# Dealing out the later groups' queries by half heads, sharing the first look-ups, and a list in two parts

## The chip, the core and the metric

The kernel runs on one core of one Trainium2 chip. The metric is the device time of one execution in microseconds. The core has five engines with a queue each: TensorE (PE: matmuls; PEld is its loading of weights), VectorE (DVE), ScalarE (ACT), GpSimd (POOL) and SyncE (SP, which here only issues DMAs). Sixteen DMA engines move the data. An engine works off its queue in order.

## The reference, cut to what matters

One layer: a modulated projection, a two-way matrix-memory scan beside attention, an output projection and a layer norm, and then a PEER layer (a product-key mixture of 16384 tiny experts) on 512 tokens. Only the PEER layer is touched by the change:

```python
q = (xt @ wq).reshape(P_BLOCK, P_HEADS, 2, P_HALF)      # 8 heads x 2 halves of 128 columns
s = jnp.einsum('nhpd,hpkd->nhpk', q, keys)              # scores against 128 keys each
s1, i1 = lax.top_k(s[:, :, 0], P_TOPK); s2, i2 = lax.top_k(s[:, :, 1], P_TOPK)
cand_s = (s1[..., :, None] + s2[..., None, :]).reshape(P_BLOCK, P_HEADS, P_TOPK * P_TOPK)
cand_i = (i1[..., :, None] * N_KEYS + i2[..., None, :]).reshape(P_BLOCK, P_HEADS, P_TOPK * P_TOPK)
top_s, pos = lax.top_k(cand_s, P_TOPK)
idx = jnp.take_along_axis(cand_i, pos, axis=-1).reshape(P_BLOCK, P_HEADS * P_TOPK)
g = jax.nn.softmax(top_s.astype(jnp.float32), axis=-1).reshape(P_BLOCK, P_HEADS * P_TOPK).astype(xt.dtype)
act = jax.nn.gelu(jnp.einsum('nd,ned->ne', xt, u[idx]), approximate=False)
return jnp.einsum('ne,ned->nd', g * act, v[idx])
```

It is done for four groups of 128 tokens.

## The kernel before

**Queries and scores.** `scores(t0, ...)` makes the scores of two groups at a time. It is a generator over 16 "heads" (8 heads x 2 halves) and one step more: a step multiplies `wq`'s 128 columns with `h2T` (8 passes over k, line 839, 16 matmul instructions as the trace counts them), copies the query to `qT` (line 841), and takes the scores of the head before (line 847). For groups 0 and 1 it runs through at once. For groups 2 and 3 it is the generator `sc1`, whose scores go through a tile `sc_` of two buffers (`to_memory`, lines 862 to 865: a copy on ScalarE, then a DMA on SP to `scd` in memory). Its last six heads read weights that lie in the three `uv` buffers of the pool `eb` (`late_rows`).

**Selection.** `select(t)` finds each token's experts on VectorE (max, index, replace; lines 896 to 980) and leaves row, column and weight in `iig`. It uses the large tile `work` as scratch. `parts` holds a later group's scores, loaded from `scd`.

**Prelude.** `prelude(t)` turns `iig` into a table of which token uses which expert, and from it into lists of rows. Three transposes `ptr` (line 1001) come first. Sixteen chunks follow (lines 1014 to 1034): VectorE builds one-hot matrices `A` and `B`, TensorE multiplies them (24 matmuls a chunk: `pf` counts, `pW` weights), ScalarE writes the weights to `work`. Then SP writes `work` to the memory table `Wd` in 16 pieces of 512 KB (line 1038; for group 0 all are sent there). From `pf` come the tables (`tables`, twice: F1 marks experts that one token uses, up to 12 blocks of 128, F2 all others), and from the tables the list: `look_up` goes through the 29 blocks in groups of three (LB): a comparison on VectorE, three matmuls `ppk`, two small VectorE instructions, and for each block a Sign on ScalarE whose accumulated sum counts how many entries lie below (line 1095). The first 12 blocks are looked up first, then tables F2, then the other 17. When all are done, three VectorE instructions (lines 1115 to 1117) make the two integer tables `ri` and `wi` of the whole list.

**The order ahead of the blocks.** A loop runs `select(0)` and `prelude(0)`, 49 steps, and after each step whose number is in HEADS it takes one step of `sc1`:

```python
    for i, _ in enumerate(chain(select(0, work), prelude(0))):
        if i in HEADS:
            next(sc1, None)
    for _ in sc1:
        pass
```

Steps 0 to 19 are the selection, 20 to 35 the chunks, 36 the first tables, 37 to 40 and 42 to 47 look-ups, 41 the second tables.

**The blocks.** `blocks` works off 4 x 29 blocks of 128 rows in a software pipeline (PIPE): `rows` gathers a block's 128 rows of `uv` (1 MB, line 1122 on GpSimd, seven buffers) and its part `wr` of `Wd`; a block of the first 12 gathers its tokens (`xg`) and takes dot products on VectorE (line 1183), one of the other 17 is transposed (`put`, line 1287) and multiplied densely (`s`, line 1301), a gelu on ScalarE and a product `wt` on VectorE (line 1303); then `py` (line 1211) adds the block up on TensorE. The order of a group's blocks is `seqs`: for groups 0 to 2 it begins with three blocks of the second part. While a group's blocks run, `select` and `prelude` of the next group are dealt out in between by a table of costs (`cost`).

The order in an engine's queue is fixed when the kernel is built, by a scheduler of the framework which starts from the order of the text and may draw an instruction forward past others that it takes to be waiting.

Of the kernel before, what the change touches and what calls it, by code (L numbers as in the profile page):

```python
# [11 lines left out]
F16 = mybir.dt.float16  # L12
I32 = mybir.dt.int32
# [6 lines left out]
P = 128  # L20
# [42 lines left out]
HEADS = (2, 4, 6, 8, 10, 12, 14, 16, 18, 21, 24, 27, 30, 33, 38, 40)  # L63
# [14 lines left out]
def tile_block(ctx, tc, xcT, x, cb, crow, w_mod1, w_modT, w_in, conv_w, conv_b, b_gates, mhw, qnw, knw,  # L78
# [748 lines left out]
    def scores(t0, late, query, score, sink):  # L827

        qs = {}
        for i in range(17):  # L830
            if i < 16:
                if i in late:
                    w = late[i]
                else:
                    w = oq.tile([P, KC, P], F32, tag="wq", name=f"wq{t0}_{i}", bufs=3)
                    nc.sync.dma_start(w, wq[:, i * P:(i + 1) * P].rearrange("(k p) n -> p k n", p=P))
                pt = query(i)
                for k in range(KC):
                    nc.tensor.matmul(pt, w[:, k, :], h2T[:, k, t0 * P:(t0 + 2) * P], start=k == 0, stop=k == KC - 1)  # L839
                qs[i] = oq.tile([P, 2 * P], F32, tag="qT", name=f"qT{t0}_{i}", bufs=2)  # L840
                nc.scalar.copy(qs[i], pt)
            if i > 0:
                j = i - 1
                qT = qs.pop(j)
                pt2 = score(j)
                for t in range(2):
                    nc.tensor.matmul(pt2[:, t * P:(t + 1) * P], qT[:, t * P:(t + 1) * P], kT[:, j, :], start=True, stop=True)
                sink(j, pt2[:, 0:2 * P].rearrange("p (t n) -> p t n", t=2))
            yield
# [31 lines left out]
    pcol = sel.tile([P, 1], F32, name="pcol")  # L881
    place = sel.tile([P, 16, 16], F16, name="place")
# [10 lines left out]
    lists = [None] * NT  # L893
# [96 lines left out]
    def prelude(t):  # L990
# [50 lines left out]
        if t == 0:  # L1041
# [5 lines left out]
        FT, jk, T0, T1, G0, G1 = (Fw[:, o:o + n] for o, n in (  # L1047
            (512, P + 2), (768, P), (1024, P + 2), (1280, P + 2), (1536, LB * P), (2048, LB * P)))
# [30 lines left out]
        def look_up(b0, b1, T, off):  # L1079
# [3 lines left out]
            for j in range(0, b1 - b0, LB):  # L1083
# [7 lines left out]
                rr = tl([P, LB], F32, f"rr{b0 + j}_", "rr", 2)  # L1091
                nc.vector.scalar_tensor_tensor(rr[:, 0:k], pk[:, 0:k, P], -1.0, plp[:, j:j + k], op0=ALU.mult, op1=ALU.add)
                nc.vector.tensor_scalar(idf[:, bs], pk[:, 0:k, P + 1], float(P), 64.0 - P, op0=ALU.mult, op1=ALU.add)
                for i in range(k):
                    nc.scalar.activation(jk, pk[:, i, 0:P], AF.Sign, scale=-1.0, bias=rr[:, i:i + 1],
                                         accum_out=kac[:, b0 + j + i:b0 + j + i + 1])
                yield

# [6 lines left out]
        yield from look_up(0, n1, T0, off1)  # L1105
# [6 lines left out]

        wi = tl([P, NBL], I32, "wi", bufs=2)
        ri = tl([P, NBL], I32, "ri", bufs=2)
        nc.vector.scalar_tensor_tensor(idf, kac, 0.5, idf, op0=ALU.mult, op1=ALU.add)
        nc.vector.tensor_copy(wi, idf)
        nc.vector.tensor_scalar_min(ri, idf, float(NEXP - 1))
        lists[t] = ri, wi
# [14 lines left out]
    def blocks(bp, eb):  # L1133
# [8 lines left out]
        def rows(t, i):  # L1142
# [6 lines left out]
            gather(w, uv, lists[t][0][:, b:b + 1])  # L1149
            wr = bp.tile([P, P], F32, tag="wr", name=f"wr{t}_{b}", bufs=LOOK + 2)  # L1150
            gather(wr, Wd[t][:, :], lists[t][1][:, b:b + 1])
# [167 lines left out]
    nc.vector.memset(onesb, 1.0)  # L1319
    nc.gpsimd.iota(pls, pattern=[[1, LB * P]], base=0, channel_multiplier=0, allow_small_or_imprecise_dtypes=True)  # L1320
# [19 lines left out]
    for _ in sc1:  # L1340
# [4 lines left out]
    cost = ([C_SEL] * 9 + [C_OH, 1.5] * 2 + [C_IIG] + [C_A] * (P // TCH) + [C_N] + [C_L] * (NB1[1] // LB) + [C_N]  # L1345
            + [C_L] * -(-(NBL - NB1[1]) // LB) + [C_N])
# [147 lines left out]
```

## Time and profile before

| what | value |
|---|---|
| median of 3 runs | 1198.37 us (1197.64 to 1202.17) |
| profiled execution | 1204.68 us, its span 1202.9 us |
| TensorE busy | 1038.4 us (86% of the span) |
| VectorE busy | 826.4 us (69%) |
| ScalarE busy | 464.8 us (39%) |
| GpSimd busy | 465.7 us (39%) |
| queries of groups 0 and 1, then 2 and 3 (TensorE) | up to 574 us |
| list of group 0 | 585 us |
| first `py` | 612 us |

A span is what the profile covers; the rest of the execution's time lies around it. Shares of busy time are means over stages of different kinds, so the rows further down are taken by stage. All times in rows are from the span's start.

### The profile page before, as it was taken

The numbers are of one execution on the slowest core, as the hardware profiler recorded it, in microseconds if no ns is written. First come the engines' busy times: TensorE is split into PE (matmuls) and PEld (weight loads), VectorE is DVE, ScalarE is ACT, GpSimd is POOL, SyncE is SP. The second block draws the span as 40 slices with busy tenths as digits, with TensorE's granted clock in tenths as the row PEclk, the third lists the DMA queues.
The fourth block names the chain that finished last, engine by engine and source line by source line (L and its number), as shares of the span: only waits on it lengthen the run. The fifth ranks groups of instructions, "written<-read, shape, count | busy, mean of one in ns | idle before, by whom it ended". The sixth has DMA issues, their size and how long they took to land.

```text
span 1202.9 us, 19211 instructions
## 1 busy us (share of the span) xinstructions
PE 1038.4 (86%) x6784; PEld 837.7 (70%) x6784; DVE 826.4 (69%) x2698; ACT 464.8 (39%) x1132; POOL 465.7 (39%) x374
## 2 busy tenths in 40 slices
PE   6889689799989999999378987989788797897985
PEld 5688678688988888898346765668555576565663
DVE  5958999869875778377795857989379785223213
ACT  3343353465562121245433454344343353522221
POOL 3643234222023520000345542656335544355760
PEclk7899899989989999999679997999899899898998
DMA  9656450220035498512978889988997877989983
GB/s 364 226 202 217 168 177 36 74 80 15 1 102 173 159 274 252 172 39 108 384 249 305 280 299 371 330 333 286 339 401 282 301 280 285 417 318 340 377 315 115
DMA packets 109038, 284.15 MB, mean 236 GB/s; under 512 B 9316, under 2 KB 62280, under 8 KB 92936
## 3 DMA queue, kind: packets, MB, share of 16 engines
q0 software_dynamic: 28048, 157.04, 35.2%
q1 hardware_dynamic: 75864, 120.32, 29.0%
q10 hardware_dynamic: 5024, 5.51, 1.3%
q8 instruction: 55, 0.90, 0.3%
q14 instruction: 47, 0.39, 0.1%
HBM read 237.17 MB, written 45.66 MB: 235 GB/s over the span
## 4 chain that ended last, share of the span: by engine, by line
PE 38%; DVE 16%; DMA 10%; issue 8%; ACT 2%; SPq 1%; POOL 1%; another core or an unknown queue 0%; DVEq 0%; ACTq 0%; POOLq 0%
PE py L1211 8%; PE pwq L839 8%; PE s L1301 4%; DMA xg<-h2d,ti 4%; PE pW L1031 3%; PE pw L770 2%; PE put L1287 2%; PE po L542 2%; DMA Wd<-work 2%; DVE work L900 2%; DMA uv<-in_uv,ri 2%; DVE work L899 1%; DVE work L902 1%; DVE work L901 1%; PE pf L1028 1%
## 5 line engine op out<-in xcount | busy, mean ns | idle before, releaser
L1211 PE MATMUL py<-uv,wt 128*128 128x512 f32 x464 | 239.7, 636 | 14.6 <-DVE wt L1303 7.8
L1122 POOL DMA_INDIRECT uv<-in_uv,ri x116 | 119.1, 1026 | 133.4 <-PE py L1211 65.0
L1301 PEld LDWEIGHTS s<-ht,ut 128*128 128x128 f32 x1088 | 141.4, 202 | 37.1 <-ACT wt L1302 18.3
L1301 PE MATMUL s<-ht,ut 128*128 128x128 f32 x1088 | 151.5, 289 | 14.8 <-ACT wt L1302 13.9
L1122 POOL DMA_INDIRECT wr<-Wd,wi x116 | 125.6, 1083 | 69.5 <-issue 35.6
L1211 PEld LDWEIGHTS py<-uv,wt 128*128 128x128 f32 x464 | 83.1, 203 | 70.0 <-issue 53.8
L1288 ACT COPY ut<-put 128x512 f32<-128x512 f32 x136 | 75.2, 588 | 102.3 <-PE put L1287 72.1
L1031 PEld LDWEIGHTS <-A 128*128 128x128 f16 x1024 | 89.7, 146 | 20.3 <-issue 13.1
L1033 ACT ACTIVATE work<-pW 128x512 f32<-128x512 f32 x128 | 73.5, 597 | 78.2 <-PE pW L1031 66.5
L1031 PE MATMUL pW<-B,A 128*128 128x128 f16 x1024 | 95.3, 225 | 6.4 <-ACT work L1033 2.9
L1287 PEld LDWEIGHTS put<-cst,uv 128*128 128x128 f32 x544 | 68.3, 152 | 41.8 <-issue 29.9
L1122 POOL DMA_INDIRECT xg<-h2d,ti x48 | 57.9, 1206 | 94.1 <-DVE ti L1163 44.6
L839 PE MATMUL pwq<-h2T,wq 128*128 128x256 f32 x416 | 94.2, 379 | 0.0
L1287 PE MATMUL put<-cst,uv 128*128 128x128 f32 x544 | 80.3, 291 | 15.4 <-DMA uv<-in_uv,ri 13.0
L1183 DVE SCALAR_TENSOR_TENSOR xg<-xg,uv 128x1024 f32<-128x1024 f32 x48 | 58.5, 1219 | 46.5 <-DMA xg<-h2d,ti 46.4
L839 PEld LDWEIGHTS pwq<-h2T,wq 128*128 128x128 f32 x416 | 77.0, 190 | 9.4
L1021 DVE TENSOR_TENSOR B<-B,igr 128x1024 f16<-128x1024 f16 x128 | 82.9, 687 | 1.0
L1018 DVE TENSOR_TENSOR A<-iob,ig 128x1024 f16<-128x1024 f16 x64 | 44.0, 688 | 47.6 <-ACT ig L1004 27.8
L1028 PE MATMUL pf<-B,A 128*128 128x128 f16 x512 | 75.0, 226 | 1.1 <-issue 1.0
L209 POOL TENSOR_TENSOR wlo<-wi,whi 128x1024 fp32r<-128x1024 f32 (+1 forms) x18 | 47.9, 2675 | 60.6 <-ACT whi L208 60.5
L1028 PEld LDWEIGHTS <-A 128*128 128x128 f16 x512 | 60.5, 147 | 8.4 <-issue 6.4
L1303 DVE TENSOR_TENSOR wt<-wt,wr 128x128 f32<-128x128 f32 x68 | 19.6, 289 | 58.1 <-ACT wt L1302 58.1
(437 smaller groups left out, 2315.8 us busy)
## 6 DMA issues: line engine op xcount, KB each, us to landing
Wd<-work SPq DMA_DIRECT2D x64, 512.0 KB
wm<-in_w_modT SPq DMA_DIRECT2D x16, 1024.0 KB
wq<-in_wq SPq DMA_DIRECT2D x26, 512.0 KB
wi<-in_w_in SPq DMA_DIRECT2D x8, 1024.0 KB
wsc<-in_w_mod SPq DMA_DIRECT2D x7, 1024.0 KB
wor<-in_w_out SPq DMA_DIRECT2D x8, 512.0 KB
wql<-in_wq SPq DMA_DIRECT2D x6, 512.0 KB
qkT<-in_w_in SPq DMA_DIRECT2D x2, 1024.0 KB
```

Source lines behind the costliest of these rows:

```text
L209: nc.gpsimd.tensor_tensor(lo[:, k:k + 4, 0:cw], wv[:, k:k + 4], hi[:, k:k + 4, 0:cw].bitcast(F32), op=ALU.subtract)
L839: nc.tensor.matmul(pt, w[:, k, :], h2T[:, k, t0 * P:(t0 + 2) * P], start=k == 0, stop=k == KC - 1)
L1021: nc.vector.tensor_tensor(B[:, q].rearrange("p a n r -> p a (n r)"), (B[:, 0] if q else ior).rearrange("p a n r -> p a (n r)"), igr[:, q, ...
L1028: nc.tensor.matmul(pf[:, 0:P], A[:, :, n], B[:, 0, :, n, :], start=c == 0 and n == 0, stop=c == P // TCH - 1 and n == TCH - 1)
L1031: nc.tensor.matmul(pw[:, (n - n4) * P:(n - n4 + 1) * P], A[:, :, n], B[:, q, :, n, :], start=q == 1, stop=q == 2)
L1033: nc.scalar.mul(Wn[:, :, n0 + n4:n0 + n4 + 4], pw.rearrange("p (n k) -> p k n", n=4), 1.0 / GSC)
L1122: nc.gpsimd.indirect_dma_start(out=dst, out_offset=None, in_=src, in_offset=bass.IndirectOffsetOnAxis(ap=ids, axis=0))
L1183: nc.vector.scalar_tensor_tensor(xg, xg, 1.0, w[:, 0:D], op0=ALU.mult, op1=ALU.mult, accum_out=nf)
L1211: nc.tensor.matmul(py[:, hs], wt, w[:, D + half * 512:D + half * 512 + 512], start=i == 0, stop=i == n - 1)
L1287: nc.tensor.transpose(pt[:, q * P:(q + 1) * P], w[:, (4 * kh + q) * P:(4 * kh + q + 1) * P], ident)
L1288: nc.scalar.copy(ut[:, 4 * kh:4 * kh + 4, :], pt.rearrange("p (q n) -> p q n", q=4))
L1301: nc.tensor.matmul(s_[:, 0:P], ut[:, k, :], ht[:, k, :], start=k == 0, stop=k == KC - 1)
```

## The change

Five edits:

- `scores` yields once more, in the middle of a query (after k = 3), so that `sc1` has 33 steps in place of 17, and HEADS has 33 numbers: nine half heads ahead of `ptr` (in place of nine heads), sixteen among the chunks (eight heads in place of five), eight among the look-ups.
- In group 0, every second group of look-ups counts on VectorE: a `scalar_tensor_tensor` that compares the same 128 numbers with the same bound, times a tile `twos` of 2.0, with an accumulated sum (15 blocks stay on ScalarE, 14 go over).
- `look_up` itself makes the integer tables of its part, `rows_of[t, b]`, in three instructions; the common ones at the end go.
- Both tables come first, then the look-ups of the 17 blocks, then those of the 12.
- The table of costs follows the new order of steps.

```diff
--- before.py
+++ after.py
@@ -60,7 +60,7 @@
 START = 6
 PIPE = (("r", 5), ("k", 4), ("u", 3), ("d", 1), ("o", 2), ("w", 1), ("h", 1), ("a", 0))
 EUV = 3
-HEADS = (2, 4, 6, 8, 10, 12, 14, 16, 18, 21, 24, 27, 30, 33, 38, 40)
+HEADS = (0, 2, 4, 6, 8, 10, 12, 14, 16) + tuple(range(20, 36)) + tuple(range(38, 46))
 SPREAD = 0.7
 OFF = 0.5
 LAG = 2
@@ -837,6 +837,8 @@
                 pt = query(i)
                 for k in range(KC):
                     nc.tensor.matmul(pt, w[:, k, :], h2T[:, k, t0 * P:(t0 + 2) * P], start=k == 0, stop=k == KC - 1)
+                    if k == KC // 2 - 1:
+                        yield
                 qs[i] = oq.tile([P, 2 * P], F32, tag="qT", name=f"qT{t0}_{i}", bufs=2)
                 nc.scalar.copy(qs[i], pt)
             if i > 0:
@@ -879,6 +881,7 @@
     iof = sel.tile([P, P], F32, name="iof")
     g2b = sel.tile([P, D], F32, name="g2b")
     pcol = sel.tile([P, 1], F32, name="pcol")
+    twos = sel.tile([P, P], F16, name="twos")
     place = sel.tile([P, 16, 16], F16, name="place")
     identb = sel.tile([P, P], F16, name="identb")
     triub = sel.tile([P, P], F16, name="triub")
@@ -890,7 +893,7 @@
     plp = sel.tile([P, NBL], F32, name="plp")
     picks = {}
     parts = {}
-    lists = [None] * NT
+    rows_of = {}
     cnt = sel.tile([1, NT], F32, name="cnt")
 
     def top16(src, n, mv_, mi_, wk):
@@ -1044,8 +1047,8 @@
 
         Fw = tl([P, 3 * P * RUN], F16, "Fw", "igr")
         F1, Fa, F2, dF = (Fw[:, i * P:i * P + P] for i in range(4))
-        FT, jk, T0, T1, G0, G1 = (Fw[:, o:o + n] for o, n in (
-            (512, P + 2), (768, P), (1024, P + 2), (1280, P + 2), (1536, LB * P), (2048, LB * P)))
+        FT, jk, T0, T1, G0, G1, jk2 = (Fw[:, o:o + n] for o, n in (
+            (512, P + 2), (768, P), (1024, P + 2), (1280, P + 2), (1536, LB * P), (2048, LB * P), (2560, P)))
         nc.vector.tensor_single_scalar(F1, pf[:, 0:P], 1.0, op=ALU.is_equal)
         nc.vector.tensor_single_scalar(Fa, pf[:, 0:P], 0.5, op=ALU.is_gt)
         idf = tl([P, NBL], F32, "idf")
@@ -1089,12 +1092,27 @@
                     nc.tensor.matmul(pk[:, i], G[:, i * P:(i + 1) * P], T, start=True, stop=True)
                 bs = slice(b0 + j, b0 + j + k)
                 rr = tl([P, LB], F32, f"rr{b0 + j}_", "rr", 2)
+                by_dve = t == 0 and j // LB % 2 == 1
                 nc.vector.scalar_tensor_tensor(rr[:, 0:k], pk[:, 0:k, P], -1.0, plp[:, j:j + k], op0=ALU.mult, op1=ALU.add)
-                nc.vector.tensor_scalar(idf[:, bs], pk[:, 0:k, P + 1], float(P), 64.0 - P, op0=ALU.mult, op1=ALU.add)
+                nc.vector.tensor_scalar(idf[:, bs], pk[:, 0:k, P + 1], float(P), (0.0 if by_dve else 64.0) - P, op0=ALU.mult,
+                                        op1=ALU.add)
                 for i in range(k):
-                    nc.scalar.activation(jk, pk[:, i, 0:P], AF.Sign, scale=-1.0, bias=rr[:, i:i + 1],
-                                         accum_out=kac[:, b0 + j + i:b0 + j + i + 1])
+                    at = kac[:, b0 + j + i:b0 + j + i + 1]
+                    if by_dve:
+                        nc.vector.scalar_tensor_tensor(jk2, pk[:, i, 0:P], rr[:, i:i + 1], twos, op0=ALU.is_lt,
+                                                       op1=ALU.mult, accum_out=at)
+                    else:
+                        nc.scalar.activation(jk, pk[:, i, 0:P], AF.Sign, scale=-1.0, bias=rr[:, i:i + 1], accum_out=at)
                 yield
+
+            n = b1 - b0
+            wi = tl([P, n], I32, f"wi{b0}_", f"wi{b0}", bufs=2)
+            ri = tl([P, n], I32, f"ri{b0}_", f"ri{b0}", bufs=2)
+            nc.vector.scalar_tensor_tensor(idf[:, b0:b1], kac[:, b0:b1], 0.5, idf[:, b0:b1], op0=ALU.mult, op1=ALU.add)
+            nc.vector.tensor_copy(wi, idf[:, b0:b1])
+            nc.vector.tensor_scalar_min(ri, idf[:, b0:b1], float(NEXP - 1))
+            for b in range(b0, b1):
+                rows_of[t, b] = ri[:, b - b0:b - b0 + 1], wi[:, b - b0:b - b0 + 1]
 
         pr, cs1, _, off1 = tables(F1, 0)
         cap = tl([P, 1], F32, "cap")
@@ -1102,20 +1120,13 @@
         nc.vector.scalar_tensor_tensor(F1, pr[:, 0:P], cap, F1, op0=ALU.is_le, op1=ALU.mult)
         nc.vector.tensor_tensor(F2, Fa, F1, op=ALU.subtract)
         yield
-        yield from look_up(0, n1, T0, off1)
         _, cs2, _, off2 = tables(F2, 1)
         pn = bank(f"pcn{t}", "p")
         nc.tensor.matmul(pn[0:1, 0:1], cs2, onesb, start=True, stop=True)
         nc.vector.tensor_scalar_add(cnt[:, t:t + 1], pn[0:1, 0:1], float(n1 * P))
         yield
         yield from look_up(n1, NBL, T1, off2)
-
-        wi = tl([P, NBL], I32, "wi", bufs=2)
-        ri = tl([P, NBL], I32, "ri", bufs=2)
-        nc.vector.scalar_tensor_tensor(idf, kac, 0.5, idf, op0=ALU.mult, op1=ALU.add)
-        nc.vector.tensor_copy(wi, idf)
-        nc.vector.tensor_scalar_min(ri, idf, float(NEXP - 1))
-        lists[t] = ri, wi
+        yield from look_up(0, n1, T0, off1)
         yield
 
     def gather(dst, src, ids):
@@ -1146,9 +1157,9 @@
                 hts[t] = channels(t, bp if t % 2 else eb)
             pool, bufs = (eb, EUV) if (t * n + i) % UVB < EUV else (bp, UVB - EUV)
             w = pool.tile([P, 2 * D], F32, tag="uv", name=f"uv{t}_{b}", bufs=bufs)
-            gather(w, uv, lists[t][0][:, b:b + 1])
+            gather(w, uv, rows_of[t, b][0])
             wr = bp.tile([P, P], F32, tag="wr", name=f"wr{t}_{b}", bufs=LOOK + 2)
-            gather(wr, Wd[t][:, :], lists[t][1][:, b:b + 1])
+            gather(wr, Wd[t][:, :], rows_of[t, b][1])
             live[t, i] = [w, wr]
 
         def token(t, i):
@@ -1317,6 +1328,7 @@
     nc.vector.memset(shiftb[:, 0:1], 0.0)
     nc.vector.tensor_copy(shiftb[:, 1:P], ident[:, 0:P - 1])
     nc.vector.memset(onesb, 1.0)
+    nc.vector.memset(twos, 2.0)
     nc.gpsimd.iota(pls, pattern=[[1, LB * P]], base=0, channel_multiplier=0, allow_small_or_imprecise_dtypes=True)
     nc.gpsimd.iota(jls, pattern=[[LB * P, 8]], base=0, channel_multiplier=0, allow_small_or_imprecise_dtypes=True)
     nc.gpsimd.iota(plp, pattern=[[P, NBL]], base=0, channel_multiplier=1, allow_small_or_imprecise_dtypes=True)
@@ -1342,8 +1354,8 @@
     ssc.close()
     sq_.close()
     sy.close()
-    cost = ([C_SEL] * 9 + [C_OH, 1.5] * 2 + [C_IIG] + [C_A] * (P // TCH) + [C_N] + [C_L] * (NB1[1] // LB) + [C_N]
-            + [C_L] * -(-(NBL - NB1[1]) // LB) + [C_N])
+    cost = ([C_SEL] * 9 + [C_OH, 1.5] * 2 + [C_IIG] + [C_A] * (P // TCH) + [C_N] * 2
+            + [C_L] * (-(-(NBL - NB1[1]) // LB) + NB1[1] // LB) + [C_N])
     whole = sum(cost)
     with tc.tile_pool(name="bp", bufs=1, reuse_waits="tile") as bp:
         n = NBL
```

## Rows read from the trace of the kernel before

**Rows 1.** Windows: us, busy (x count) by engine, PE clock, DMA share, GB/s
```profile
482.00:518.00 36.00, 35.97 (x186) 32.20 (x187) 11.14 (x52) 7.49 (x23) 0.56 (x1) 1.00 0.55 161
518.00:566.00 48.00, 47.86 (x501) 44.03 (x500) 42.58 (x81) 25.21 (x48) 0.00 (x0) 1.00 0.10 34
566.00:585.00 19.00, 10.26 (x68) 7.60 (x66) 10.56 (x74) 14.31 (x63) 0.59 (x1) 0.77 1.01 389
585.00:621.00 36.00, 18.50 (x86) 14.43 (x86) 31.80 (x197) 9.65 (x16) 18.69 (x18) 0.65 0.83 313
621.00:768.00 147.00, 129.75 (x914) 95.93 (x915) 106.40 (x423) 61.36 (x169) 70.84 (x67) 0.93 0.86 310
```

**Rows 2.** Waits, 482 to 585: who waited for whom, total, times, longest
```profile
DVE A L1018 <- ACT ig L1004: 24.6, 1, 24.6
```

**Rows 3.** Timeline of VectorE, five stretches: start, us, instruction, idle before
```profile
493.39 0.22 DVE L959 TENSOR_TENSOR iig<-work 128x64 f32<-128x64 f16 x1
...
562.88 0.29 DVE L1049 TENSOR_SCALAR Fw<-pf 128x128 f16<-128x128 f32 x1 [2.15 <-PE pf L1028]
...
565.62 0.35 DVE L1102 SCALAR_TENSOR_TENSOR Fw<-ppr,cap,Fw 128x128 f16<-128x128 f32 x1
...
579.66 0.47 DVE L898 MAX8 work<-scfx 128x8 f32<-128x128 f32 x2
...
584.86 0.17 DVE L1117 TENSOR_SCALAR ri<-idf 128x29 int32<-128x29 f32 x1
...
733.85 0.49 DVE L898 MAX8 work<-scfx 128x8 f32<-128x128 f32 x2 [4.64 <-DMA Wd<-work]
```

**Rows 4.** Timeline of TensorE, 513 to 751
```profile
513.34 3.62 PE L839 MATMUL pwq<-h2T,wq 128*128 128x256 f32 x16
...
517.24 0.49 PE L1001 MATMUL ptr<-cst,iig 128*128 128x128 f32 x3
...
517.56 3.19 PE L839 MATMUL pwq<-h2T,wq 128*128 128x256 f32 x14
...
520.59 0.98 PE L1028 MATMUL pf<-B,A 128*128 128x128 f16 x13
...
573.65 0.44 PE L847 MATMUL psc<-kT,qT 128*128 128x128 f32 x2
...
611.98 3.78 PE L1211 MATMUL py<-uv,wt 128*128 128x512 f32 x4 [2.76 <-DVE wt L1303]
...
621.40 3.70 PE L1211 MATMUL py<-uv,wt 128*128 128x512 f32 x8 [0.72 <-DVE wt L1303]
...
750.60 1.94 PE L1287 MATMUL put<-cst,uv 128*128 128x128 f32 x8 [2.27 <-DMA uv<-in_uv,ri]
```

**Rows 5.** Chain that ended last, one piece: start, us, what
```profile
529.24 0.92 PE pW L1031 x15
```

**Rows 6.** Timeline of GpSimd, 585 to 894
```profile
585.31 1.00 POOL L1122 DMA_INDIRECT uv<-in_uv,ri  x1 [10.10 <-DVE work L900]
...
586.62 0.97 POOL L1122 DMA_INDIRECT uv<-in_uv,ri  x1 [0.30 <-DMA Wd<-work]
...
744.82 0.94 POOL L1122 DMA_INDIRECT uv<-in_uv,ri  x1 [14.45 <-PE put L1287]
...
893.68 1.00 POOL L1122 DMA_INDIRECT uv<-in_uv,ri  x1 [4.35 <-PE s L1301]
```

**Rows 7.** Lines by form, 482 to 590: count, busy us, mean ns, idle
```profile
L1095 ACT ACTIVATE Fw<-ppk,rr 128x128 f16<-128x128 f32 x29 | 10.7, 370 | 4.3 <-PE ppk L1089 2.0 <-DVE idf L1093 1.6
...
L1095 ACT ACTIVATION_READ_ACCUMULATOR Fw<-ppk,rr 128x1 f32 x29 | 5.7, 196 | 0.0
```

**Rows 8.** Timeline of SP's queue, 560 to 640
```profile
563.63 18.84 SPq L1038 DMA_DIRECT2D Wd<-work  x16
...
582.57 2.78 SPq L865 DMA_DIRECT2D scd<-sc  x2
```

**Rows 9.** Timeline of ScalarE at 595
```profile
595.11 0.38 ACT L864 COPY sc<-psc 128x256 f32<-128x256 f32 x1
```

## Prediction

> **What bounds the kernel now.** Start with the busy time by stage [rows 1]. From 482 to 566 us TensorE is busy in 83.8 of 84 us at the full granted clock: it is the bound there. From 566 to 585 it is busy 10.3 of 19 while the DMA engines are full (share 1.01, 389 GB/s). From 585 to 621 TensorE does 18.5 of 36 at a mean granted clock of 0.65, and VectorE is busy 31.8 of 36. After 621 the blocks run with TensorE at 88% and the DMA engines at 0.86; the last stage is a mixture.
>
> Next the waits of 482 to 585 [rows 2]: VectorE sits idle 24.6 us before its first A. The timelines say why. VectorE wrote the last of iig at 493.4 to 493.6 [rows 3], but the transposes ptr that need it ran on TensorE at 517.24, right behind a head of group 2's queries that began at 513.34 [rows 4]. Nine heads are dealt ahead of ptr in the text, and TensorE works them off first. One head (16 matmuls of the query, then the scores of the head before) takes 517.24 - 513.34 = 3.90 us.
>
> From ptr to the end of the sixteen chunks (F1 reads pf at 562.88, after a wait of 2.15 us for TensorE [rows 3]) is 45.6 us. A chunk's matmul takes 0.92/15 = 61 ns [rows 5], so 16 chunks x 24 matmuls are 23.5 us; the five heads dealt there are 19.5; the sum is 43.0, and 2.6 is start-up and waits. TensorE's last score of the dealt queries ends at 574.1 [rows 4]. The numbers ri of the first list are there at 585.0 [rows 3], and GpSimd gathers at 585.31 [rows 6]. In that tail ScalarE goes through 29 look-ups, 0.37 us for a Sign and up to 0.20 for its sum [rows 7], and TensorE has nearly nothing to do.
>
> Meanwhile SP issues the sixteen pieces of Wd, from 563.63 over 18.84 us [rows 8]; 8.4 MB at 389 GB/s are 21.6 us, which fits GpSimd's release at 586.62 [rows 6]. VectorE begins select(1) at 579.66 [rows 3], and the first py comes at 611.98, the next at 621.40, both released by wt on VectorE [rows 4].
>
> Last, the change from group 0 to group 1 [rows 6]: GpSimd stood 14.45 us before the gather at 744.82 and 4.35 at the next change of groups. There the list of a whole group is finished at once, after look-ups that queue on VectorE behind a select which waited 4.64 us for Wd at 733.85 [rows 3].
>
> **The change part by part.** *Half heads.* Ahead of ptr stand 4.5 heads in place of 9: 4.5 x 3.90 = 17.5 us less, ptr at 499.7, and iig has been ready since 493.6, so TensorE still sets it. But the sixteen chunks now carry 8 heads in place of 5: 31.2 + 23.5 + 2.6 = 57.3 us, and they end at 557.0. VectorE is no obstacle: it needed 42.6 us busy in the old stage and gets 57. Net, 1.5 heads were put off: 5.9 us earlier. Bounds: 17.5 if the later heads cost nothing there, 0 if the queue comes out as it was. I take 5.9, since the rows show TensorE full on both sides.
>
> The 3.5 heads put off, and the last score, need 14.1 us after the chunks. Before, from 562.9 to 574.1, TensorE did two heads and the last score (8.2) and 3.0 us of tables and look-ups. Now it has both tables and eight or more of ten look-up groups in that time, some 5.5 us. So it ends at about 557.0 + 19.6 = 576.6. The queries end 2.5 us later than before, which hurts only those who wait for their buffers.
>
> *Look-ups shared.* ScalarE keeps 15 of 29: 15 x 0.57 = 8.5 us at most, where it had 16.4. VectorE gets 14, priced by the nearest row, a scalar_tensor_tensor of 128x128 out of PSUM at 0.35 us [rows 3]: 4.9 us; the bounds are 0 (in its idle time: it was busy 10.6 of 19) and 14 x 0.57 = 8.0. Either lies inside TensorE's 19.6, and I cost them at nothing; without that cover they would be 4.9.
>
> *Two parts with their own numbers.* The first three blocks of groups 0 to 2 are of the second part, which now is looked up first. In group 0 its last look-up stands behind five half heads: 557.0 + 9.75 + about 4 for tables and look-ups + 1.5 for comparisons and three conversions = 572; the first part follows at 576.6 + 1.5 = 578. Against 585.0 that is 13 and 7 us earlier. Each list has three more instructions of 0.17 us, nine in the later groups, 1.5 us on VectorE in all, hidden because VectorE is not full there (106 of 147 us); uncovered they cost 1.5. The memset of twos, and the yield in the first two groups' queries, cost nothing.
>
> *What can use it.* Wd's writes start 5.9 us earlier and alone would end at 580.7. A gather uv is 1.05 MB, 2.7 us at 389 GB/s; three that go out from 572 on run beside the writes, so Wd's last piece lands between 580.7 and 588.8, against 586.6. The Trainium skill ("DMA: Bandwidth & Descriptors", section "Queues, rings and completion order") says that a DMA engine takes turns between the queues that have work, a packet at a time; by that the later end, 588.8, holds. No row here shows the two side by side; the row on the full engines [rows 1] agrees that what one gets the other loses. wr, and select(1), which overwrites `work`, wait for those writes. For the first blocks I take the 5.9 by which the whole stage is early. Bounds: 13 (the list) and -2 (Wd by turns).
>
> *Later groups.* The first three gathers of a group no longer wait for the twelve look-ups of the other part. Bounds: 0, and 14.45 + 4.35 = 18.8 us. But behind the longer wait TensorE itself lacked rows for 2.27 us only [rows 4], and the DMA engines have 14% free over that group [rows 1]. I take 3 us for the three changes of groups together, near the 2.27.
>
> The sum is 5.9 + 3 = 8.9. The profiled execution took 1204.68 us, a span of 1202.9 and 1.8 around it, 0.5% above the median of 1198.37. 1204.68 - 8.9 = 1195.8; at the scale of the median, **1189.5 us**. About 0.5%, 6 us, is what a measurement of this kernel can tell from no change.
>
> **The rivals.** *(a) SP's queue eats it.* A head's scores go to scd through SP and two buffers. Three scores used to come after Wd's pieces were queued, now five. The two after Wd are issued only when its sixteen pieces are (582.57 [rows 8]), and the third copy, whose buffer waits for them, came at 595.11 [rows 9]. Now three copies, not one, wait so, from 557.8 + 18.8 = 576.6 on. Each holds the one bank that scores and `s` share, so queries end near 584 and not 576.6; buffers laid over them come free 10 us later than before, and Signs queued behind a copy on ScalarE push the first part's list to about 588. Then only the later groups gain: 1198.4 - 3 = 1195.4. For it: the order of the queue is in the rows. Against: in the old trace ScalarE went on with other work before that copy.
>
> *(b) More than forecast.* Between 585 and 621 half of TensorE's time is lost because wt waits in VectorE's queue behind select(1). If rows 13 us earlier bring the first wt ahead of it, some 8 of the 17.5 idle us come back too: 1198.4 - 17 = 1181.
>
> *(c) Slower.* Early gathers push Wd out, in every group: 3 x 2.7 = 8.1 us on the writes, for which select of the next group waits, with look-ups and wt queued behind it on VectorE (the 4.64 us at 733.85 [rows 3]). At 8.1 in each of the three groups with a select to follow, 24.3 - 8.9 = 15.4 slower: 1213.8; at 4 us each, 1201.5. It decides from 3 us a group on. The rule of turns just named is its ground. Against: those DMA bytes must be moved anyway.
>
> *(d) It does not do what it says.* The queues are not quite in the order of the text: 14 matmuls of head 9 ran at 517.56, ahead of the first chunk's pf at 520.59, though dealt after it [rows 4]. If heads are drawn forward past ptr as well, ptr stays near 517 and only the later groups gain: 1195.4.
>
> **How the numbers follow.** Forecast 0.43, (a) 0.22, (b) 0.18, (c) 0.10, (d) 0.07. The forecast's own range is 1186 to 1194: six sevenths of it lie below 1192.4, 0.36 faster and 0.07 same. (b) is faster, 0.18. (a) and (d) are same but for 0.04 that come out lower: 0.25 same, 0.04 faster. Of (c) 0.07 are slower and 0.03 same. Faster 0.58, same 0.35, slower 0.07. The range of 1178 to 1199 reaches from below (b) to above (a) and leaves out most of (c) and the low end of (b), about 0.15.
>
> **What would show it.** Right: ptr near 500; F1 near 557; VectorE's wait before the first A from 24.6 to some 7 us; first gather near 572; the whole first stage of blocks 6 us early; the wait before the first gather of group 1 gone or short. Wrong: ptr near 517 (d); copies of scores on ScalarE that wait past 580 with Signs behind them (a); a longer wait of select for Wd in groups 1 and 2 (c); a first py well before 606 with TensorE full from then on (b).

## The result, and the profile of the changed kernel

The changed kernel is slower: 1204.76 us (median of 20) against 1198.26 us (20), a ratio of 1.0058, 95% interval 1.0039 to 1.0076: 0.58%, or 6.5 us. The forecast was 1189.5 us, with a range of 1178 to 1199 and a chance of 0.07 for slower.

The windows of the changed kernel by stage (us, busy time of each engine, granted clock of TensorE, DMA share, GB/s), beside [rows 1]:

```profile
518.00:566.00 48.00, 48.00 (x425) 42.68 (x424) 31.04 (x86) 21.06 (x50) 0.00 (x0) 1.00 0.34 126
566.00:585.00 19.00, 8.15 (x48) 6.62 (x46) 5.58 (x38) 4.76 (x20) 5.69 (x6) 0.71 0.98 377
585.00:621.00 36.00, 26.96 (x125) 20.58 (x126) 28.36 (x189) 9.26 (x20) 18.66 (x21) 0.77 0.85 304
621.00:768.00 147.00, 121.87 (x874) 89.22 (x873) 111.58 (x450) 62.15 (x166) 66.95 (x60) 0.93 0.81 295
```

TensorE's and VectorE's timelines and one row of VectorE's waits show that the first stage came out early, as forecast and better:

```profile
498.29 0.49 PE L1004 MATMUL ptr<-cst,iig 128*128 128x128 f32 x3
604.27 2.18 PE L1222 MATMUL py<-uv,wt 128*128 128x512 f32 x4
```

```profile
DVE A L1021 <- ACT ig L1007: 6.8, 1, 6.8
```

The transposes run at 498.29 (517.24 in [rows 4]), VectorE's wait before the first A falls from 24.6 [rows 2] to 6.8, the chunks end at 553, and the first py comes at 604.27 (611.98 in [rows 4]). TensorE does 26.96 us of work from 585 to 621, where it did 18.50. But in the 19 us before that, from 566 to 585, VectorE is busy for only 5.58 (10.56 in [rows 1]). Its timeline says why, and GpSimd's says where the wait comes from:

```profile
575.41 0.17 DVE L1113 TENSOR_SCALAR ri<-idf 128x12 int32<-128x12 f32 x1
590.26 0.49 DVE L901 MAX8 work<-scfx 128x8 f32<-128x128 f32 x2 [14.68 <-DMA scfx<-scd]
```

```profile
570.28 1.10 POOL L1133 DMA_INDIRECT uv<-in_uv,ri  x1 [139.08 <-DMA Wd<-work]
...
572.94 0.94 POOL L1133 DMA_INDIRECT uv<-in_uv,ri  x1 [0.30 <-issue]
581.69 0.95 POOL L1133 DMA_INDIRECT wr<-Wd,wi  x1 [7.81 <-DMA Wd<-work]
...
584.19 0.94 POOL L1133 DMA_INDIRECT wr<-Wd,wi  x1 [0.30 <-issue]
585.13 0.60 POOL L1251 DMA_DIRECT2D scfx<-scd  x1
585.72 0.58 POOL L1251 DMA_DIRECT2D scfy<-scd  x1
586.60 0.99 POOL L1133 DMA_INDIRECT uv<-in_uv,ri  x1 [0.30 <-issue]
```

VectorE finishes the list at 575.6 and then stands still for 14.68 us, for the scores of group 1. Their load `scfx`, `scfy` is issued on GpSimd's queue, and there it now stands behind three gathers of uv and three of wr, of which the first wr waits 7.81 us for Wd. In the kernel before, GpSimd issued the same load ahead of every gather:

```profile
461.73 0.74 POOL L1240 DMA_DIRECT2D scfx<-scd  x1 [29.07 <-DMA wql<-in_wq]
486.57 0.56 POOL L1240 DMA_DIRECT2D scfy<-scd  x1 [24.10 <-DMA scd<-sc]
```

In the text of both kernels this load stands behind the gathers of the first three blocks (it is due in the third turn of `blocks`). In the kernel before, the scheduler drew it forward past them; in the changed kernel it stays where the text has it. Why the scheduler treated it otherwise, no run shows.

So select(1) begins at 590.26 in place of 579.66 [rows 3], though the list ahead of it is done 9 us earlier. What rival (a) foresaw is there too: SP's queue holds the last five writes of scores behind the pieces of Wd, and copies on ScalarE wait.

```profile
553.87 17.58 SPq L1041 DMA_DIRECT2D Wd<-work  x16
571.54 20.39 SPq L867 DMA_DIRECT2D scd<-sc  x5
```

```profile
585.51 0.37 ACT L866 COPY sc<-psc 128x256 f32<-128x256 f32 x1 [11.31 <-DMA scd<-sc]
...
591.18 0.37 ACT L866 COPY sc<-psc 128x256 f32<-128x256 f32 x1 [3.61 <-DMA scd<-sc]
```

At the change to group 1 the second part's numbers come 34.1 us after the end of that group's chunks (702.95), and before the whole list came 38.7 after it (705.32 to 744.05). The first part's numbers come 41.9 after it, later than the whole list before. The lead of the second part is no larger because on VectorE its numbers stand behind select(2), which waits for Wd. That wait is 6.70 (4.64 in [rows 3]), but a second trace of the kernel before, e8_before, has 7.05, so the two can't be told apart. GpSimd's wait is 12.0 (14.45 in [rows 6]), with one more after it:

```profile
734.47 0.49 DVE L901 MAX8 work<-scfx 128x8 f32<-128x128 f32 x2 [6.70 <-DMA Wd<-work]
736.89 0.17 DVE L1113 TENSOR_SCALAR ri<-idf 128x17 int32<-128x17 f32 x1
```

```profile
737.82 0.94 POOL L1133 DMA_INDIRECT uv<-in_uv,ri  x1 [11.99 <-issue]
742.60 0.94 POOL L1133 DMA_INDIRECT uv<-in_uv,ri  x1 [3.85 <-PE py L1222]
```

The two profiled executions have equal spans (1202.9 and 1202.8), since the one of before lay 6 us above its own median. The verdict rests on the medians, the reading on the order of events.

### The profile page after: what moved, and what is told of

The parts are those of the page before. It is cut to its first block, busy times and chain, and to the rows that moved or that the text cites. A ratio compares the mean times of both kernels' runs of the same rounds, so it can differ in the third digit from the quotient of the medians.

```text
span 1202.8 us, 19211 instructions
## 1 busy us (share of the span) xinstructions
PE 1034.9 (86%) x6784; PEld 834.1 (69%) x6784; DVE 830.8 (69%) x2739; ACT 459.4 (38%) x1104; POOL 467.4 (39%) x374
## 4 chain that ended last, share of the span: by engine, by line
PE 39%; DMA 11%; DVE 10%; issue 9%; ACT 3%; POOL 2%; another core or an unknown queue 1%; SPq 0%; DVEq 0%; ACTq 0%; POOLq 0%
PE pwq L839 8%; PE py L1222 8%; PE s L1312 5%; DMA xg<-h2d,ti 4%; PE pW L1034 3%; PE put L1298 3%; PE pw L770 2%; DMA Wd<-work 2%; PE po L542 2%; DMA scd<-sc 2%; DMA uv<-in_uv,ri 1%; PE pf L1031 1%; PE psc L849 1%; PE ppt L568 1%
## 5 line engine op out<-in xcount | busy, mean ns | idle before, releaser
L1222 PE MATMUL py<-uv,wt 128*128 128x512 f32 x464 | 238.8, 633 | 18.9 <-DVE wt L1314 9.1
L1133 POOL DMA_INDIRECT uv<-in_uv,ri x116 | 126.1, 1087 | 270.3 <-DMA Wd<-work 139.1
L1133 POOL DMA_INDIRECT wr<-Wd,wi x116 | 121.1, 1044 | 102.5 <-issue 31.4
L1298 PEld LDWEIGHTS put<-cst,uv 128*128 128x128 f32 x544 | 64.6, 146 | 37.2 <-issue 23.5
L219 PE MATMUL pn<-wlo,hhi 128*128 128x256 f32 (+1 forms) x176 | 50.9, 289 | 0.8 <-POOL wlo L209 0.7
```

Source lines behind the costliest of these rows:

```text
L219: nc.tensor.matmul(pt, a_, b_, start=k == 0 and q == 0, stop=k == KC - 1 and q == 2)
L1133: nc.gpsimd.indirect_dma_start(out=dst, out_offset=None, in_=src, in_offset=bass.IndirectOffsetOnAxis(ap=ids, axis=0))
L1222: nc.tensor.matmul(py[:, hs], wt, w[:, D + half * 512:D + half * 512 + 512], start=i == 0, stop=i == n - 1)
L1298: nc.tensor.transpose(pt[:, q * P:(q + 1) * P], w[:, (4 * kh + q) * P:(4 * kh + q + 1) * P], ident)
```

## The experiments

They ran in four sets on chips that take some 1180 us for the kernel before. Each set timed the kernel before beside its own runs; its medians were 1180.24, 1180.82, 1180.20 and 1179.60 us, in the order of the runs below. Prices are differences of ratios to it; 0.1% is 1.2 us. The sets ran on three chips (the second and the last on one), so most prices between runs of two sets also compare two chips. e8_before, one execution on the chip of the second set, gave a trace of the kernel before and no price.

| run | what | us | against before, 95% interval |
|---|---|---|---|
| e1_heads | before + half heads | 1188.78 | +0.76% (+0.49 to +1.02) |
| e2_noheads | changed, whole heads | 1185.06 | +0.40% (+0.12 to +0.67) |
| e3_late | before + late load | 1194.72 | +1.39% (+1.08 to +1.70) |
| e4_earlyB | changed + early load | 1174.42 | -0.52% (-0.75 to -0.29) |
| e5_h_early | half heads + early load | 1170.30 | -0.94% (-1.28 to -0.61) |
| e6_list0 | e4, old list in groups 1 to 3 | 1176.06 | -0.48% (-0.73 to -0.22) |
| e7_scact | e4, last scores by ScalarE's queue | 1178.93 | -0.14% (-0.39 to +0.12) |
| e9_hold | e4, first gathers held for Wd | 1179.04 | -0.05% (-0.26 to +0.17) |
| e10_nodve | e4, look-ups all on ScalarE | 1167.95 | -1.12% (-1.43 to -0.81) |
| e11_h_dve | e5, look-ups shared | 1171.57 | -0.72% (-1.00 to -0.45) |
| e12_list | before + list in two parts | 1182.71 | +0.08% (-0.20 to +0.37) |
| e13_after | the changed kernel | 1187.07 | +0.59% (+0.30 to +0.88) |
| e14_nodve | changed, look-ups all on ScalarE | 1183.41 | +0.29% (+0.09 to +0.49) |
| e15_earlyB | as e4 | 1173.08 | -0.48% (-0.69 to -0.27) |
| e16_early_nodve | as e10 | 1169.80 | -0.99% (-1.33 to -0.64) |

**The late load.** Half heads alone:

```diff
-HEADS = (2, 4, 6, ..., 38, 40)
+HEADS = (0, 2, 4, ..., 16) + tuple(range(20, 36)) + tuple(range(38, 46))
+                    if k == KC // 2 - 1:
+                        yield
```

> The kernel before with the half heads alone (the other list of places and the second yield; look-ups and list as they were). Theory A, the late load: GpSimd issues the load of group 1's scores behind the first gathers, so VectorE starts select(1) near 590 us instead of 579.7 although the chunks end near 553; the first stage's gain of some 8 us is lost again there, and the kernel is 3 to 9 us slower than before. Rival B, the score copies behind Wd on SP's queue: the copies on ScalarE wait past 585 us, select(1) starts early, and the time is within 2 us of before. Rival C, the loss comes from the list in two parts in the later groups: then this run gains the 5.9 us that were forecast for the stage.

```profile
583.73 0.61 POOL L1242 DMA_DIRECT2D scfx<-scd  x1
```

```profile
591.15 0.49 DVE L900 MAX8 work<-scfx 128x8 f32<-128x128 f32 x2 [15.70 <-DMA scfx<-scd]
```

It is the half heads that put the load behind the gathers: with them alone, `scfx` is issued at 583.73 behind three wr, select(1) begins at 591.15, and the kernel is 0.76% (9 us) slower. Theory A holds; B and C would have been near zero or faster.

Late load alone, on the kernel before:

```diff
+                if t == 1:
+                    for q in range(2):
+                        nc.vector.tensor_copy(parts[t][q][:, 0:1], lists[0][0][:, 0:1])
```

> The kernel before with one thing added: VectorE writes one column of the two tiles for group 1's scores from the finished numbers ri, so that GpSimd can issue their load only behind the first gathers. Nothing else is later. Theory A: select(1) starts near 590 us instead of 579.7, the first stage of blocks has the same start, and the kernel is 5 to 10 us slower. Rival D, VectorE has room until the next change of groups, so that a select that starts 10 us later costs nothing: within 2 us of before.

```profile
591.07 0.61 POOL L1243 DMA_DIRECT2D scfx<-scd  x1
```

```profile
597.92 0.49 DVE L898 MAX8 work<-scfx 128x8 f32<-128x128 f32 x2 [15.34 <-issue]
```

With the queue's order changed in this one point, select(1) begins at 597.92, 17.5 us after the 580.42 of e8_before (20.7 counted from the end of the chunks), and the time rises by 1.39%, 16.4 us. That is more than the 5 to 10 expected; select(1) also came later than the 590 expected. The first py is not late (606.54 against 608.08 in e8_before), so it is the late select(1) that reaches the end, and most of its delay does. Rival D falls.

Early load, on the changed kernel (the tiles are the two buffers of B, idle after the chunks; the loads stand in the text ahead of the gathers):

```diff
+        if t == 0:
+            parts[1] = []
+            for q in range(2):
+                B = tl([P, 3, P // RUN, TCH, RUN], F16, f"sc{q}_", "B", 2)
+                B = B.rearrange("p q a n r -> p (q a n r)").bitcast(F32)[:, 0:D]
+                nc.gpsimd.dma_start(B, scd[1, :, q * D:q * D + D])
+                parts[1].append(B)
...
-        loads = {DEFER - LOOK: 1, AT: 2, n + AT: 3}
+        loads = {AT: 2, n + AT: 3}
```

> The changed kernel with the load of group 1's scores issued on GpSimd's queue right after the sixteen chunks, ahead of all gathers, into the two buffers of B that lie idle then. Theory A: select(1) starts at 575 to 579 us, right behind the list, and the kernel is 5 to 10 us faster than before, 11 to 16 faster than the changed one. Rival B or C (score copies, or the later groups): select(1) starts early all the same and the time stays 4 us or more above before; 1 MB more ahead of Wd would cost 2.7 us at most.

```profile
547.45 0.74 POOL L1049 DMA_DIRECT2D sc<-scd  x1 [118.36 <-PE pW L1034]
551.13 0.56 POOL L1049 DMA_DIRECT2D sc<-scd  x1 [2.94 <-DVE Fw L1058]
567.25 1.00 POOL L1139 DMA_INDIRECT uv<-in_uv,ri  x1 [15.56 <-DVE work L901]
```

```profile
566.80 0.17 DVE L1119 TENSOR_SCALAR ri<-idf 128x17 int32<-128x17 f32 x1
566.88 0.48 DVE L901 MAX8 work<-sc 128x8 f32<-128x128 f32 x2
```

```profile
566.00:585.00 19.00, 5.84 (x34) 4.46 (x32) 18.85 (x137) 3.02 (x14) 2.91 (x3) 0.67 0.92 373
```

The load goes out at 547 and 551, select(1) begins at 566.88, right behind the second part's numbers and ahead of most look-ups of the first part, so earlier than the 575 to 579 expected, and VectorE is busy 18.85 of the 19 us in which it did 5.58. The kernel is 0.52% faster than before, as theory A has it; B and C expected it slower. That the place of the load turns the sign was seen again with both kernels on one chip:

> The changed kernel once more, on one chip with the three runs below, so that the price of the late load and that of the shared look-ups are read from runs of one call. Theory A: 4 to 10 us slower than before, select(1) near 590 us after a wait of some 14 us.

> The changed kernel with the early load, as before: 5 to 8 us faster than the kernel before, and 10 to 15 us faster than the changed kernel of this call (theory A).

1187.07 against 1173.08 us: 1.07%, 12.6 us by the ratios. In these two traces the last iig of select(1) starts at 640.38 and 621.49, 18.9 apart. By the end of group 1's chunks (699.84 and 690.63) half of that is left, 9.2; it then stays, since the last py ends at 1169.56 and 1160.13, 9.4 apart.

**The list in two parts, and the later groups.**

```diff
-HEADS = (0, 2, 4, ..., 16) + tuple(range(20, 36)) + tuple(range(38, 46))
+HEADS = (2, 4, 6, ..., 38, 40)
```

> The changed kernel with the queries dealt out as before (whole heads, the old places); shared look-ups and the list in two parts stay. Theory A: the load of group 1's scores goes out ahead of the gathers again (before 490 us), select(1) starts no later than 579.7, and the list's gain shows: 2 to 6 us faster than before. Rival C, early gathers push Wd out and the later groups lose: as slow as the changed kernel, 4 to 8 us slower than before.

Slower by 0.40% where theory A had it faster, although the load went out early: something else in the change costs. In the trace select(2) waits for Wd with the numbers behind it:

```profile
732.72 0.49 DVE L899 MAX8 work<-scfx 128x8 f32<-128x128 f32 x2 [15.10 <-DMA Wd<-work]
...
735.14 0.17 DVE L1111 TENSOR_SCALAR ri<-idf 128x17 int32<-128x17 f32 x1
```

From it came theory L, tried from two sides:

> Half heads and the early load of group 1's scores alone: look-ups all on ScalarE and the list as before. Theory L, the list in two parts costs time in the later groups (there select of the next group waited 15.1 us for Wd in the run with whole heads, and the second part's numbers stood behind it): without it 3 to 6 us faster than the half heads with early load and the list in two parts, so 8 to 12 us faster than before. Rival M, the list in two parts gains in the first group and what that run lost came by another way: 0 to 5 us slower than with it, so 1 to 6 us faster than before.

> The changed kernel with the early load, and with the list in two parts in group 0 alone; groups 1 to 3 look up the first part first and take their numbers together, as before. Theory L: the wait of select(2) for Wd falls back to some 5 us, and the kernel is 8 to 12 us faster than before. Rival M, the loss lies in group 0 (part two first, shared look-ups): it stays where half heads with early load and the list in two parts everywhere were, 4 to 7 us faster than before.

```diff
         yield
+        if t > 0:
+            yield from look_up(0, n1, T0, off1)
         _, cs2, _, off2 = tables(F2, 1)
...
+        if t == 0:
+            numbers(n1, NBL)
+            yield from look_up(0, n1, T0, off1)
+            numbers(0, n1)
+        else:
+            numbers(0, NBL)
```

e5_h_early (all of the list and the look-ups as before) gained what L said, but e6_list0, which has the old list in groups 1 to 3, came out like e4_earlyB: -0.48 and -0.52%, though its select(2) waits only 4.09 us for Wd (6.71 in e4_earlyB). These two could hide some 4 us, the interval of their difference; L falls with them and with e10_nodve and e16_early_nodve below, which have the list in two parts in every group and are as fast as e5_h_early. The loss lies in group 0. (`numbers` holds what `look_up` does after its loop.)

**Wd pushed out, or the look-ups on VectorE.** In e4_earlyB Wd's last piece lands at 584.64, 33.9 us after the chunks, with three gathers issued from 567.25; in e5_h_early at 578.78, 26.6 after, with the gathers from 576.25. The fourth gather is issued at 589.17 and 583.83. Theory W held the gathers back:

```diff
+            if t == 0 and i < 3:
+                nc.gpsimd.dma_start(w[:, 0:1], Wd[0][0:NEXP, :].rearrange("(a k) n -> a k n", k=P)[:, P - 1, P - 1:P])
             gather(w, uv, rows_of[t, b][0])
```

> The changed kernel with the early load, and with the first three gathers of uv in group 0 held until the last piece of Wd is written: ahead of each, one column of its tile is read from the last piece's rows. Theory W, the three early gathers take the DMA engines from Wd (Wd's last piece landed at 584.6 with them, at 578.8 in the half heads with early load and the old list) and the fourth gather, behind wr on GpSimd's queue, is 5 us late for it: Wd lands near 579 again, the fourth gather comes before 587, and the kernel is 3 to 6 us faster than the early load alone, 8 to 12 us faster than before. Rival S, the loss lies in the look-ups on VectorE or in the list's order, not in the gathers: within 2 us of the early load alone, or slower, since the first rows come 8 us later.

```profile
578.82 1.62 POOL L1167 DMA_DIRECT2D uv<-Wd  x3 [26.06 <-DMA Wd<-work]
581.73 1.01 POOL L1139 DMA_INDIRECT uv<-in_uv,ri  x1 [1.29 <-DVE work L901]
...
589.33 0.94 POOL L1139 DMA_INDIRECT uv<-in_uv,ri  x1 [0.30 <-issue]
```

Wd landed at 578.3, as W said, but the fourth gather stayed at 589.33 and the first three came 14 to 17 us later: 0.47% slower than e4_earlyB. Theory W had it faster and fails on the time. Early gathers do push Wd out in these kernels, and are still worth having. How far they push it hangs on how much of Wd is left when they start. In the changed kernel no early load stands ahead of Wd: 7.8 MB have gone by SP's queue 20 us after the chunks (e13_after), where it is 6.8 in e4_earlyB. There Wd's last piece lands 28.2 us after the chunks in e13_after and 23.8 in e14_nodve, with three early gathers in both, and 24.7 in e1_heads without them. The look-ups, next:

```diff
-                by_dve = t == 0 and j // LB % 2 == 1
+                by_dve = False
```

> The changed kernel with the early load, and with all look-ups of group 0 on ScalarE again; half heads and list in two parts stay. Rival S: without the look-ups on VectorE it is 3 to 6 us faster than with them, 8 to 12 us faster than before. Theory W: the second part's numbers still come 7 us or more ahead of Wd's end, the gathers still push it out, and it is 4 to 7 us faster than before, as with the shared look-ups.

> Half heads, early load and the list of before as one, with the look-ups of group 0 shared between ScalarE and VectorE: the whole list near 572 instead of 576. Theory W: three gathers from 572 on push Wd out by some 3 to 4 us, and the run lies between the two: 6 to 10 us faster than before. Rival S (look-ups on VectorE cost 5 us): 4 to 6 us faster than before.

> The kernel before with the list in two parts alone (whole heads, look-ups on ScalarE). Theory W: with whole heads too, three gathers go out ahead of Wd's end and push it out: 2 to 6 us slower than before, as the run that had the shared look-ups as well (4.8 slower). Rival S: within 2 us of before, and the 4.8 us belong to the look-ups on VectorE.

> The changed kernel with all look-ups of group 0 on ScalarE, the load of group 1's scores late as in the changed kernel. Theory S, the look-ups on VectorE cost 2 to 7 us by themselves: that much faster than the changed kernel of this call. Rival N, what looked like their price is chance or the order of the queues that goes with one build: within 2 us of it.

> Half heads, the list in two parts and the early load, look-ups all on ScalarE. Theory S: 3 to 7 us faster than the same with shared look-ups in this call, 9 to 13 us faster than before. Rival N: within 2.5 us of it.

Five pairs differ in the shared look-ups alone. The last column is how many us later select(1)'s last iig ends, counted from the end of the chunks:

| with and without | price | iig of select(1) |
|---|---|---|
| e2_noheads, e12_list | +0.32% | +3.3 |
| e4_earlyB, e10_nodve | +0.60% | +2.3 |
| e11_h_dve, e5_h_early | +0.22% | +2.1 |
| e13_after, e14_nodve | +0.30% | +3.6 |
| e15_earlyB, e16_early_nodve | +0.51% | +2.8 |

All have one sign, and the mean is 0.39%, 4.6 us. Alone only the two pairs with 0.60 and 0.51% are clear of their intervals, some 0.4% either way; the first three pairs also compare two chips. S holds and N falls by the five together. e11_h_dve by itself, 8.5 us faster than before, lies in W's range and not in S's.

The pairs don't all lose by the same way. In the fourth, select(1) already starts 3.6 us later (38.2 against 34.6 after the chunks), since its load stands behind the wr, which come later with Wd: there the whole +3.6 is the later load, and from its start to its last iig select(1) takes as long (49.1 and 49.2). In the other four it starts at most 0.7 later; from there to the last iig VectorE is busy 1.2 to 2.3 us longer, and idle by between 0.6 less and 1.2 more.

The list in two parts shows neither cost nor gain: +0.08% alone, and -1.12 and -0.99% with half heads and early load against -0.94% without it.

**The score copies.** The last five heads' scores written from ScalarE's queue:

```diff
-        nc.sync.dma_start(scd[t:t + 2, :, j * P:(j + 1) * P].rearrange("t p n -> p t n"), sc_)
+        (nc.scalar if j > 10 else nc.sync).dma_start(scd[t:t + 2, :, j * P:(j + 1) * P].rearrange("t p n -> p t n"), sc_)
```

> The changed kernel with the early load, and with the last five heads' scores written to scd from ScalarE's own queue, so that they don't stand behind the sixteen pieces of Wd. Theory B, the copies that wait (12.7 us on ScalarE, up to 585 us, with the copies of ut behind them) hold back the first blocks: the first py comes 3 to 6 us before 599 and the time falls by 2 to 5 us below the 5.8 us that the early load alone is faster than before. Rival: the first blocks wait for their rows beside Wd anyway, and VectorE's select goes on as it did: within 1.5 us of the early load alone.

```profile
578.23 0.37 ACT L866 COPY sc<-psc 128x256 f32<-128x256 f32 x1 [5.68 <-DMA scd<-sc]
```

```profile
581.82 0.93 POOL L1139 DMA_INDIRECT uv<-in_uv,ri  x1 [8.39 <-DVE work L904]
592.53 0.95 POOL L1139 DMA_INDIRECT wr<-Wd,wi  x1 [9.79 <-DMA scfx<-scd]
```

```profile
580.52 0.17 DVE L1117 SCALAR_TENSOR_TENSOR idf<-kac,idf 128x12 f32<-128x12 f32 x1 [3.89 <-ACT Fw L1111]
```

The copies were done by 578.6 (588.8 in e4_earlyB), but the first py came hardly earlier: 600.97 against 599.05, or 47.5 against 48.3 us after the chunks. Two queues were built in another order. GpSimd's has a fourth uv ahead of the first wr, which went out 7 us later (4.4 counted from the chunks). On ScalarE the last three Signs stand behind the copy that waited until 578.23, so VectorE stood 3.89 us and select(1) with it; its last iig ends 10 us later, counted from the chunks. The run is 0.38% slower than e4_earlyB, against both expectations. So it doesn't tell what the copies would give with the queues as they were; that is left open.

Half heads, the list in two parts and the early load, without the shared look-ups, beat both kernels: -1.12% and -0.99% against before.

## Why the prediction was wrong

**The step that failed** is "For the first blocks I take the 5.9 by which the whole stage is early", with the sentence ahead of it: "wr, and select(1), which overwrites `work`, wait for those writes". select(1) was taken to be ready once the list and Wd were. It also needs its scores, whose load stands on GpSimd's queue, and that queue was read in the prediction for its gathers only. With half heads the load stays behind the gathers (e1_heads). The first py did come 7.7 us earlier, but select(1) began 10.6 us later, and the kernel's time went with select(1). Price by e13_after and e15_earlyB: 1.07%; alone on the kernel before (e3_late): 1.39%. The other half of the sentence was wrong as well: with its scores there, select(1) of e4_earlyB begins at 566.88, 18 us before Wd's last piece lands. The rows of the kernel before had it so already, with select(1) at 579.66 [rows 3] and Wd's end put at 586.62.

**Half heads, -5.9 forecast.** The mechanism was right, the size too small. The chunks ended at 553.1 and not 557.0, 9.8 us earlier than before: the transposes came 1.4 earlier than forecast, and from them to the end of the chunks it took 54.8 us and not 57.3. With the load early (e5_h_early) the kernel gained 0.94%, 11 us; select(1) began 12.8 us earlier than in the kernel before (567.61 against 580.42) and filled VectorE's idle tail.

**Look-ups shared, 0 forecast, 4.9 without cover.** The cover was VectorE's idle time, which is just what an earlier select(1) uses up. Measured: 4.6 us in the mean, with select(1) done 2.1 to 3.6 us later. That it lies near 4.9 proves little, since the pairs go from 0.22 to 0.60%. In the changed kernel itself VectorE was idle after the list, and what they delayed was the load, by way of Wd and the wr (e13_after, e14_nodve). In the other pairs VectorE's own time is 1.2 to 2.3 us of it. How the rest of the price arises is not settled.

**The list, 13 and 7 us earlier.** The parts were done at 569.4 and 575.6, 16 and 9 earlier (forecast 572 and 578). But three gathers then share the DMA engines with Wd: it lands 31.5 to 33.9 us after the chunks in five runs with the list in two parts and the early load (e4, e6, e10, e15, e16), 26.6 in the two with the list as one (e5, e11). The rule of turns in the Trainium skill ("DMA: Bandwidth & Descriptors", section "Queues, rings and completion order") agrees with this sharing; that the turns are a packet long, no run here shows. Gain in time: none that can be told (e12_list, +0.08%).

**Later groups, -3 forecast.** No gain shows: e6_list0 and e4_earlyB differ by 0.04%, though with an interval of some 0.34% either way they can't rule 3 us out. The numbers of the second part don't wait for the look-ups of the first any more, but in the changed kernel and in e2_noheads they stood behind select of the next group, which waits for Wd, and those of the first part came later than the whole list before.

**The sum.** -0.94% for half heads, 0 for the list, +0.39 for the shared look-ups, +1.07 for the late load make +0.52%; measured +0.58% and +0.59%. The 1.07 is itself the difference of e13_after and e15_earlyB, so the sum tests only the rest: -0.55 against the -0.48 of e15_earlyB.

**The rivals.** (a) was right that the copies wait, but not that this decides the time: in e4_earlyB they wait until 588.8 too, and it is faster than before. What they cost is open. (b) saw that more than 5.9 us was there to be had, by another way than wt ahead of select(1). (c) named the right side and the right queue on VectorE, select with look-ups and wt behind it, but not the load, and the longer wait of select(2) for Wd that it named can't be told from the 7.05 of e8_before. (d) fell: the transposes moved. Slower was given 0.07, since no rival asked what else select(1) reads.

## What to carry to other kernels

When a stage is made to end earlier, list every operand of the instruction that is to profit, and find for each one where its load stands in its queue. A queue whose order is made by a scheduler can change in places that the edit doesn't touch; here a load that the scheduler used to draw forward stayed behind gathers that wait. Idle time that covers one part of a change may be what another part of it fills: cost them together.

## What was not expected of the hardware

Nothing of the chip itself was unexpected but the size of what sharing costs. Three gathers of 1.05 MB, by estimate 8.1 us of the DMA engines at the 389 GB/s of [rows 1], put Wd's end off by 5 to 7 us in the runs with the early load, and by between nothing and 3.5 in the two of the changed kernel's kind, where less of Wd was left when they began (e13_after and e14_nodve, against e1_heads). Holding them back cost 0.47% in the one run that did (e9_hold).
